# State-space steps of two groups taken as a pair, in a hybrid gMLP and Mamba-2 block

## The chip, the cores and the metric

The kernel runs on one core of one Trainium2 chip, in one launch. The metric is the device time of an execution in microseconds (us). An engine here is TensorE (PE, with its weight loads PEld), VectorE (DVE), ScalarE (ACT), GpSimd (POOL) or SyncE (SP); "SPq" and "ACTq" mark the instructions by which SP and ACT issue transfers.

## The reference

One layer of a trunk with two parallel branches, on x of 1024 positions by 1024 channels, in float32:

```python
h = rms_norm(x, norm_w) * (1 + scale) + shift          # scale, shift, gate from silu(c) @ ada_w + ada_b
gm_u, gm_v, gm_z, ssm_z, xbc, dt_raw, g_a, g_b = split(h @ w_in)
y_a = spatial_gating(gelu(gm_u), gelu(gm_v), ...) * silu(gm_z)
xs, bm, cm = split(silu(causal_depthwise_conv(xbc, conv_w, conv_b)))
dt = softplus(dt_raw + dt_bias);  a = -exp(a_log)
y_b = ssd_scan(xs, dt, a, bm, cm) + xs * d_skip         # 8 groups of 4 heads of 64, state 128, chunks of 128
y_b = rms_norm(y_b * silu(ssm_z))                       # by group of 256 channels
out = rms_norm(x + gate * ((sigmoid(g_a) * (y_a @ w_proj_a) + sigmoid(g_b) * (y_b @ w_proj_b)) @ w_out))
```

The part that the change touches is `ssd_scan`. For each group, chunk by chunk, with `decay` the masked exponential of differences of the cumulated `dt * a`:

```python
cb      = C_chunk @ B_chunk^T                           # 128 x 128, one for the group's 4 heads
y_diag  = (cb * decay[head]) @ xd[head]                 # inside the chunk
state   = state * chunk_decay + B_chunk^T @ (decay_to_end * xd)
y_off   = (C_chunk @ state_before) * exp(a_cs)          # from earlier chunks
```

## The kernel before

**Layout.** Everything is kept transposed, channels on partitions and positions along the free axis. The large projections are float32 products split into high and low parts (three products each) and combined in a scheme of seven products in place of eight. The state-space part comes near the end of the program, from about 920 to 1130 us. It is followed by the projection of branch B (tiles `x0p`, `x1p`, ..., the first of which are fed by `yn0`, `yn1`, ... on lines 1614 and 1651) and the output projection.

**One step.** A step is a group g and a pair of chunks s (256 positions). There are 8 groups and 4 pairs of chunks, so 32 steps. `order` runs them in rounds of two groups: (0,0), (1,0), (0,1), (1,1), (0,2), ... In the profile a tile's name has no numbers; in the order lists `yi5_0` is the tile of group 5, pair of chunks 0. A step does this:

- `fetch`: SP loads `dcy` (cumulated sums, spread over partitions, 512 KB) and `sl` (the slabs of C, B, x and gate, 768 KB). Five sets of buffers rotate.
- `mask`, `decay`: ACT makes `ea` (exponentials for y_off), POOL masks `dcy` (L1123), and ACT takes the eight exponentials of `dcy` (L1131).
- `prep`: PE makes `pc` (C·B, and B transposed) and `px` (x transposed). DVE multiplies `dcy` by `pc` (L1147) and makes `xd` and `xe` from `px` (L1150). ACT copies `bn`.
- `front`: PE makes `yi` (the part inside the chunk, eight products that are 64 columns wide, so that two heads share a bank), and `sp` (two increments of the state). DVE adds an increment to the state that POOL has multiplied by the chunk's decay (`st`, L1192 and L1200), and adds the skip term to `yi` (`y`, L1180).
- `back`: PE makes `yn` from the earlier states. DVE multiplies it by `ea` (`ym`, L1226), POOL adds and gates (L1228, L1229).

After each second step of a group, ACT stores the gated tile `yz` to `yb_d` (L94) and later squares it in place, so the squares wait until the store has read it. POOL adds the two halves (L1255 `sum`, or L1247 in `late_squares` for the last two groups), PE sums over partitions with a matrix of ones (`pq`, 32 columns wide), DVE scales the row (`cwt` or `tri`), ACT stores it to `ms_d`, SP loads it back as `ssq`, and POOL raises it to the power -1/2 (`root`).

**What fills PE between.** `proj_a`, the projection of branch A, is a generator of units, each of two 128x512 products (tiles `pma`). `draw(n)` takes n units. Its results are gated on DVE (`tha`, L1488) and stored by ACT to `mt_d` (L1490).

**What sets the order.** A scheduler places instructions, but the lists are mostly fixed by hand: `link` chains the instructions of ACT, DVE and POOL in the order in which they are written, products and loads are pinned in program order, `later(d, f)` runs f after d more calls of `run_tasks`, and `work` holds POOL's sums and roots, one of which `beside_step` takes. PSUM is eight banks: `bank` takes each from a ring of six (`bk`), or, every fourth time, from a ring of two (`px`). The loop over steps writes front, state product, fill, back, prep of step n+2, fetch of step n+5:

## Time and profile before

| | |
|---|---|
| Time, median of 3 runs | 1369.64 us (1369.3 to 1369.72) |
| The profiled execution | 1367.94 us, of which the span of the profile is 1366.0 us |
| Granted TensorE clock of that execution | 0.999 |
| PE busy | 1352.3 us (99%) |
| PEld, DVE, ACT, POOL busy | 82%, 77%, 59%, 14% of the span |
| Instructions of the span | 20176 |

Busy time is the share of a span in which an engine has an instruction running; the rows of the trace give for each group of instructions the start, the duration, the engine, the line, and the tiles as out<-in. Duration and distance from one start to the next are not the same: PE, DVE and ACT start an instruction while the one before is still ending. A matmul of float32 operands appears as two records, so the eight products of a `yi` are 16 records. Brackets name the idle time ahead of a row and what ended it. The profiled execution is 1.70 us under the median of the timed runs.

### The profile page before, as it was taken

How to read it: one execution, taken by the hardware profiler on the slowest of the kernel's cores; microseconds unless marked ns; L12 is line 12 of the kernel's file. 1: busy time of each engine (PE TensorE's matmuls, PEld its weight loads, DVE VectorE, ACT ScalarE, POOL GpSimd, SP SyncE). 2: the span in 40 equal slices, each digit the busy share in tenths (PEclk: the TensorE clock that was granted, in tenths of full speed). 3: DMA queues.
4: the chain of work that ended last, by engine and by line, in shares of the span. 5: the costliest groups of instructions: out<-in, count | busy, mean ns of one | idle time of the engine just before them, and what ended most of it. 6: DMA issues, size and time to landing. Idle time of an engine off the chain costs nothing.

```text
span 1366.0 us, 20176 instructions
## 1 busy us (share of the span) xinstructions
PE 1352.3 (99%) x6943; PEld 1116.6 (82%) x6943; DVE 1045.9 (77%) x1716; ACT 799.2 (59%) x1447; POOL 192.5 (14%) x191
## 2 busy tenths in 40 slices
PE   8999999999999999999999999999999999999997
PEld 7688888888888888888888888888888887888886
DVE  4786876777778888697887797458888866859976
ACT  5763666666666656466566556486877834233443
POOL 1000000000000000000000000006798971000002
PEclk9999999999999999999999999999999999999999
DMA  9674444334344657877656675589889959988903
GB/s 286 181 244 135 142 124 120 104 117 124 108 139 139 181 181 230 252 230 241 211 180 189 219 247 167 166 282 314 305 299 307 309 201 320 325 268 322 382 37 124
DMA packets 249530, 288.65 MB, mean 211 GB/s; under 512 B 16812, under 2 KB 196436, under 8 KB 249428
## 3 DMA queue, kind: packets, MB, share of 16 engines
q1 hardware_dynamic: 174868, 203.80, 46.9%
q10 hardware_dynamic: 74560, 83.57, 17.9%
q8 instruction: 55, 0.90, 0.3%
q14 instruction: 47, 0.39, 0.1%
HBM read 199.82 MB, written 87.49 MB: 210 GB/s over the span
## 4 chain that ended last, share of the span: by engine, by line
PE 92%; DMA 3%; DVE 2%; ACT 1%; SPq 1%; issue 0%; POOL 0%; POOLq 0%; DVEq 0%; ACTq 0%
PE xz L565 6%; PE xcb L565 6%; PE xx L565 6%; PE pma L82 6%; PE xuz L565 6%; PE xg L565 6%; PE ox L1867 3%; PE ycb L565 3%; PE vx L954 3%; PE yp L1676 3%; PE yz L565 3%; PE yx L565 3%; PE yg L565 3%; PE yuz L565 3%; PE yi L82 2%; PE sp L82 2%
## 5 line engine op out<-in xcount | busy, mean ns | idle before, releaser
L1123 POOL TENSOR_SCALAR_AFFINE_SELECT dcy<-dcy 128x1024 f32<-128x1024 f32 x32 | 35.3, 1103 | 790.6 <-ACT ea L1119 786.9
L1131 ACT ACTIVATE dcy<-dcy,nacs 128x128 f32<-128x128 f32 x256 | 78.3, 389 | 2.7 <-POOL dcy L1123 2.1
L1147 DVE TENSOR_TENSOR dcy<-dcy,pc 128x1024 f32<-128x1024 f32 x32 | 39.0, 1218 | 8.0 <-PE pc L85 6.4
L1229 POOL TENSOR_TENSOR yz<-y,sl 128x512 f32<-128x512 f32 x32 | 44.4, 1387 | 2.5
L82 PE MATMUL pma<-yh,wah 128*128 128x512 f32 x128 | 43.1, 418 | 0.0
L82 PE MATMUL pma<-yh,wal 128*128 128x512 f32 x128 | 42.5, 413 | 0.0
L82 PE MATMUL pma<-yl,wah 128*128 128x512 f32 x128 | 40.2, 396 | 0.0
L1119 ACT ACTIVATE ea<-dcy 64x512 f32<-64x512 f32 x64 | 39.8, 622 | 0.7 <-DMA dcy<-acs_d 0.3
L1024 ACT ACTIVATE ac<-ac 128x1024 f32<-128x1024 f32 x32 | 33.9, 1061 | 10.2 <-DVE ac L1022 10.0
L1614 DVE SCALAR_TENSOR_TENSOR yn<-yn,par,rb 128x512 f32<-128x512 f32 x32 | 25.4, 793 | 18.6 <-DMA yn<-yb_d 16.9
L1154 ACT COPY bn<-pc 128x256 f32<-128x256 f32 x32 | 11.9, 371 | 46.9 <-DVE dcy L1147 46.9
L1228 POOL TENSOR_TENSOR y<-y,ym 128x512 f32<-128x512 f32 (+1 forms) x32 | 37.0, 1155 | 1.9 <-DVE ym L1226 1.9
L1022 DVE SCALAR_TENSOR_TENSOR ac<-c2x,cwt,ac 128x1023 f32<-128x1023 f32 (+2 forms) x24 | 30.7, 1279 | 6.1 <-ACT ac L1020 6.0
L82 PE MATMUL yi<-dcy,xd 128*64 128x128 f32 x512 | 35.0, 279 | 0.0
L1022 DVE SCALAR_TENSOR_TENSOR ac<-c2cb,cwt,ac 128x1023 f32<-128x1023 f32 (+2 forms) x24 | 30.6, 1274 | 5.6 <-ACT ac L1020 5.5
L1882 POOL TENSOR_TENSOR r<-r,fnw 128x512 f32<-128x512 f32 x4 | 5.3, 1344 | 204.8 <-ACT junk L1880 204.8
L986 ACT ACTIVATE vm<-vm,vr 128x128 f32<-128x128 f32 x64 | 25.8, 484 | 14.2 <-DMA vm<-v_d 13.7
L1226 DVE TENSOR_TENSOR ym<-yn,ea 128x512 f32<-128x512 f32 (+1 forms) x32 | 19.9, 622 | 18.5 <-PE yn L82 18.4
L824 ACT CAST wbb<-wbr 128x512 fp32r<-128x512 f32 x32 | 19.8, 619 | 22.8 <-DMA wb_d<-wbb 17.0
L82 PE MATMUL sp<-xe,bn 128*128 128x256 f32 x112 | 32.7, 409 | 0.0
L82 PEld LDWEIGHTS yn<-sl,st 128*128 128x128 f32 x224 | 29.7, 191 | 2.8 <-POOL st L1192 0.4
L82 PEld LDWEIGHTS yi<-dcy,xd 128*64 128x64 f32 x512 | 27.3, 136 | 5.7 <-issue 3.1
(2963 smaller groups left out, 4372.8 us busy)
## 6 DMA issues: line engine op xcount, KB each, us to landing
sl<-s_d SPq DMA_DIRECT2D x32, 768.0 KB, 6.4
s_d<-ac ACTq DMA_DIRECT2D x32, 512.0 KB, 3.3
wb_d<-wbb ACTq DMA_DIRECT2D x32, 512.0 KB, 3.4
dcy<-acs_d SPq DMA_DIRECT2D x32, 512.0 KB, 5.3
av<-in_w_in_dram SPq DMA_DIRECT2D x36, 256.0 KB, 2.9
aw<-in_ada_w_dram SPq DMA_DIRECT2D x16, 512.0 KB, 6.6
wbr<-in_w_proj_b_dram SPq DMA_DIRECT2D x32, 256.0 KB, 5.1
yb_d<-yz ACTq DMA_DIRECT2D x32, 256.0 KB, 6.0
```

The lines of the kernel that those rows point to most:

```text
L82: pin(PE.matmul(acc, l, r, start=first, stop=last))
L565: pin(PE.matmul(ps, lw[:, k * P : (k + 1) * P], r[k], start=first and n + k == 0, stop=n == 2 and k == 3, skip_group_check=not first))
L954: pin(PE.matmul(ps[pn][j], l[:, j * P : (j + 1) * P], r, start=nm in ("p1", "p5", "p2") and n + units[i][1] == 0, stop=n == 2 and k == 3, ...
L1022: V.scalar_tensor_tensor(ac[:, s:], cc[:, : S - s], conv_wt[:, 3 - s, i : i + 1], ac[:, s:], op0=ALU.mult, op1=ALU.add)
L1119: link("A", lambda: A.activation(ea[hh * HD : (hh + 1) * HD], dcy.rearrange("p (j e) i l -> p e j (i l)", e=2)[hh * HD : (hh + 1) * HD, hh ...
L1123: link("G", lambda: G.affine_select(out=d8, in_=d8, compare_op=ALU.is_ge, fill=-1e30, base=0, pattern=[[0, 2 * HPG], [1, P]], channel_mult ...
L1131: link("A", lambda: A.activation(dcy[:, h, i, :], dcy[:, h, i, :], AF.Exp, bias=sub[:, i, h : h + 1]))
L1147: link("V", lambda: V.tensor_tensor(d3, d3, pc[:, 0:256].unsqueeze(1).to_broadcast([P, HPG, 256]), op=ALU.mult))
L1228: link("G", lambda: G.tensor_add(y1[:, :, t0:], y1[:, :, t0:], m[:, :, t0:]))
L1229: link("G", lambda: G.tensor_mul(yz, y1, sl[:, 4:6]))
L1676: pin(PE.matmul(ps[j], a[:, v, js], r, start=first and n + k == 0, stop=n == 2 and k == KT - 1, skip_group_check=not first))
L1867: pin(PE.matmul(ps, a[:, tsl], b[:, cs], start=first and n + j == 0, stop=n == 2 and j == 3, skip_group_check=not first))
```

## The change

Steps n and n+1 (the same pair of chunks of both groups of a round) are taken as one. `fronts` writes, on every engine's list, the inside products of both, then both rows of sums (`pq`), both increments, both skips, both first state additions, then the second state product and addition of the first group (`second`). POOL's sums or roots follow, two in a row, and the fill. `backs` writes both `yn` with the second group's second state product between, and both state products for the next pair. `preps` writes both `prep` of the next pair, both pairs of `ea` exponentials, both masks, and only then both `xe` (`prep2`). `fetch` is split: the loads of sums (`dcy`) are issued in `fronts`, those of `sl` at the pair's end. The squares come six slots after the store in place of eight, and the names of three PSUM banks of the next stage change places. No instruction is added or removed.

```diff
@@ fetch, exps, mask @@
-        def fetch(self, s):
-            g, nm = self.g, f"{self.g}_{s}"
-            n = nstep[0] % NSET
+        def fetch_sums(self, s):
...
+        def fetch(self, s):
...
+        def exps(self, s):
@@ prep @@
-            for v, f in (("xd", dthq), ("xe", dde)):
+            xd = scaled("xd", dthq)
...
+            self.rest = lambda: scaled("xe", dde)
+
+        def prep2(self, s):
+            self.pre[s][4] = self.rest()
@@ front, cut in three: inside (yi), increments (sp), skip (y) @@
-        def front(self, s):
+        def inside(self, s):
...
+        def increments(self, s):
...
+        def skip(self, s):
@@ post @@
-                later(8, self.squares, q, [yz[:, j] for j in range(2)])
+                later(6, self.squares, q, [yz[:, j] for j in range(2)])
@@ the loop @@
-    draw(6)
-    for n in range(2):
-        step(n, "front")
-        ahead_of(n)
-        draw(10)
-    for n in range(len(order)):
-        if n > 1:
-            step(n, "front")
-            ahead_of(n)
-            draw(6 if n == 2 else 4 + n % 2)
-        step(n, "back")
-        if n == 1:
-            draw(4)
-        if n + 2 < len(order):
-            step(n + 2, "prep")
-        fetch(n + 6)
+    def fronts(n):
+        decays(n + 4)
+        each(n, "inside")
+        while posts:
+            p, q, sq = posts.pop(0)
+            p.post2(q, sq)
+        each(n, "increments")
+        each(n, "skip")
+        each(n, "add_state", 0)
+        second(n)
+        upto("fetch_sums", n + 7)
+    def second(n):
+        g, s = order[n]
+        if s < NCH // 2 - 1:
+            groups[g].mul_state(s, 1)
+            groups[g].add_state(s, 1)
+    def backs(n):
+        for m in (n, n + 1):
+            g, s = order[m]
+            groups[g].back(s)
+            if m == n:
+                second(n + 1)
+            groups[g].close(s)
+        if n + 2 < len(order) and order[n + 2][1]:
+            each(n + 2, "mul_state", 0)
+    def preps(n):
+        for m in (n, n + 1):
+            if m < len(order):
+                g, s = order[m]
+                groups[g].prep(s)
+                upto("exps", m + 3)
+        upto("mask", n + 4)
+        each(n, "prep2")
+    draw(12)
+    for n in range(0, len(order), 2):
+        item(fronts, n)
         with tc.high_priority():
-            decays(n + 3)
...
+            for _ in range(2 if n < 28 else 4):
                 beside_step()
+        draw(4 if n == 0 else 3)
+        item(backs, n)
+        item(preps, n + 2)
+        upto("fetch", n + 7)
+        run_tasks()
+        draw(12 if n == 0 else 6 + n // 2 % 3 % 2)
+        run_tasks()
```

**PE, the step of group 4 and of group 5 at pair of chunks 0.** Before, from the products inside the chunk of step (5,0) to the next such products; `pq3_0` is a row of sums of group 3, `pma4_0` and `pma4_1` are fill, and eight fill rows like the two shown stand between them and `yn5_0`:

```order
L82 MATMUL yi5_0_9725<-dcy5_0_9403,xd5_0_9627 64x128 x8
L82 MATMUL pq3_0_9734<-yz3_0_9119,ones_140 32x128 x4
L82 MATMUL sp5_0_9741<-xe5_0_9629,bn5_0_9631 128x256 x2
L82 MATMUL pma4_0_9683<-yh10_8034,wah4_0_9361 128x512
L82 MATMUL pma4_1_9686<-yh11_8035,wah4_0_9361 128x512
```

Now, the same place:

```order
L82 MATMUL yi4_0_9647<-dcy4_0_9201,xd4_0_9578 64x128 x8
L82 MATMUL yi5_0_9656<-dcy5_0_9377,xd5_0_9596 64x128 x8
L82 MATMUL pq2_0_9665<-yz2_0_9064,ones_140 32x128 x4
L82 MATMUL pq3_0_9672<-yz3_0_9072,ones_140 32x128 x4
L82 MATMUL sp4_0_9679<-xe4_0_9609,bn4_0_9580 128x256 x2
L82 MATMUL sp5_0_9682<-xe5_0_9611,bn5_0_9598 128x256 x2
```

Both groups' narrow products stand in a row, as do both rows of sums and both pairs of increments. After them come 6 fill products, both `yn`, both `pc` and `px`, and 12 or 14 more fill products.

**SP, the loads ahead of group 5's first step.** Before (`ssq<-ms_d0` and `ssq<-ms_d1` read back the sums of groups 0 and 1):

```order
L91 DMA ssq_158<-ms_d0_66 128x8
L91 DMA dcy4_0_9315<-acs_d_57 128x1024
L91 DMA sl4_0_9317<-s_d4_125 128x1536
L91 DMA ssq_158<-ms_d1_67 128x8
L91 DMA dcy5_0_9403<-acs_d_57 128x1024
L91 DMA sl5_0_9405<-s_d5_126 128x1536
```

Now:

```order
L91 DMA dcy5_0_9377<-acs_d_57 128x1024
L91 DMA dcy4_1_9379<-acs_d_57 128x1024
L91 DMA ssq_158<-ms_d0_66 128x8
L91 DMA ssq_158<-ms_d1_67 128x8
L91 DMA sl5_0_9463<-s_d5_126 128x1536
L91 DMA sl4_1_9465<-s_d4_125 128x1536
```

The load of `sl4_0` has moved ahead of both reads of sums; `sl5_0` and `sl4_1` stand behind both. The next round has the same piece with groups 7 and 6.

**DVE and ACT at the stage's end.** On DVE, from the last `ym` (group 7, pair 3), before; `yn0_0` on line 1614 is the first operand of projection B, normalised after a load from `yb_d`:

```order
L1226 TENSOR_TENSOR ym7_3_10842<-yn7_3_10837,ea7_3_10531 128x512
L1488 SCALAR_TENSOR_TENSOR tha6_0_10576<-tha6_0_10576,pma6_0_10578 128x512
L1488 SCALAR_TENSOR_TENSOR tha6_1_10579<-tha6_1_10579,pma6_1_10581 128x512
L1267 TENSOR_SCALAR cwt_148<-pq6_0_10863 128x128
L1267 TENSOR_SCALAR tri_142<-pq7_0_10870 128x128
L1614 SCALAR_TENSOR_TENSOR yn0_0_10922<-yn0_0_10922,par2_147,rb0_0_10920 128x512
```

Now:

```order
L1239 TENSOR_TENSOR ym7_3_10831<-yn7_3_10826,ea7_3_10582 128x512
L1658 SCALAR_TENSOR_TENSOR yn0_0_10922<-yn0_0_10922,par2_147,rb0_0_10920 128x512
L1506 SCALAR_TENSOR_TENSOR tha6_0_10603<-tha6_0_10603,pma6_0_10605 128x512
L1506 SCALAR_TENSOR_TENSOR tha6_1_10606<-tha6_1_10606,pma6_1_10608 128x512
L1280 TENSOR_SCALAR cwt_148<-pq6_0_10871 128x128
L1280 TENSOR_SCALAR tri_142<-pq7_0_10878 128x128
```

`yn0_0` has moved ahead of the two `tha6`. On ACT, before, from the stores of group 6's last tile:

```order
L94 DMA yb_d12_103<-yz6_2_10679 128x512
L94 DMA yb_d13_104<-yz6_2_10679 128x512
L1490 DMA mt_d6_89<-tha6_0_10576 128x512
L1490 DMA mt_d6_89<-tha6_1_10579 128x512
L1268 DMA ms_d6_72<-cwt_148 4x128
L94 DMA yb_d14_105<-yz7_2_10749 128x512
L94 DMA yb_d15_106<-yz7_2_10749 128x512
L1268 DMA ms_d7_73<-tri_142 4x128
L1246 ACTIVATE yz6_2_10679<-yz6_2_10679 128x512 x2
```

Now:

```order
L1508 DMA mt_d6_89<-tha6_0_10603 128x512
L94 DMA yb_d12_103<-yz6_2_10704 128x512
L94 DMA yb_d13_104<-yz6_2_10704 128x512
L1508 DMA mt_d6_89<-tha6_1_10606 128x512
L1259 ACTIVATE yz6_2_10704<-yz6_2_10704 128x512
L1281 DMA ms_d6_72<-cwt_148 4x128
L94 DMA yb_d14_105<-yz7_2_10714 128x512
L94 DMA yb_d15_106<-yz7_2_10714 128x512
L1259 ACTIVATE yz6_2_10704<-yz6_2_10704 128x512
```

The store of the first `tha6` stands ahead of the stores of `yz6`, and the first square of `yz6` ahead of the stores of `yz7`.

More of the change, by code (lines that the diff above doesn't have):

```diff
@@ L1320, in start_ssd @@
             later(4 + 5 * n, decays, n + 1)
-            g, s = order[n]
-            later(13 + n, groups[g].prep, s)
+            later(13 + n, prep, n)
     def stats():
@@ L1797, in hybrid_kernel @@
             if nm == "p1":
-                first = {t: psb.tile([P, 512], F32, name=f"{t}p", tag=f"b{t}") for t in ('x0', 'x1', 'x2', 'y3', 'y0', 'y1', 'y2', 'x3')}
+                first = {t: psb.tile([P, 512], F32, name=f"{t}p", tag=f"b{t}") for t in ('x0', 'x1', 'x2', 'y2', 'y0', 'y3', 'y1', 'x3')}
                 psx, psy = ([first[f"{v}{j}"] for j in range(4)] for v in "xy")
```

106 lines of the change are left out of this document (52 added, 54 removed).

## The prediction

> **What bounds the kernel now.** I read the page first, then PE's waits, then single steps on PE, then each place where the change writes a wait that is not there today. The page's busy line and its chain of waits:
>
> ```profile
> PE 1352.3 (99%) x6943; PEld 1116.6 (82%) x6943; DVE 1045.9 (77%) x1716; ACT 799.2 (59%) x1447; POOL 192.5 (14%) x191
> PE 92%; DMA 3%; DVE 2%; ACT 1%; SPq 1%; issue 0%; POOL 0%; POOLq 0%; DVEq 0%; ACTq 0%
> ```
>
> PE is the bound. PE's waits over the whole state-space stage and its end (935 to 1140 us) are one row:
>
> ```profile
> PE pq L82 <- POOL yz L1247: 1.4, 2, 0.8
> ```
>
> So nothing in the steps holds PE up. It waits twice at the end, 1.4 us in all, for POOL's add of the last squares. Two things follow. A reordering can gain only what PE itself spends on the order of its products, and 1.4. And every wait that it writes into PE's list is paid in full, since PE has no idle time to absorb it.
>
> **What PE spends on changes of shape.** The timeline of PE in one step, as start, duration and records (two records to a product):
>
> ```profile
> 1042.36 1.05 PE L82 MATMUL yn<-sl,st 128*128 128x128 f32 x8
> 1043.25 0.39 PE L82 MATMUL pc<-sl 128*128 128x128 f32 x2
> ...
> 1044.13 0.38 PE L85 MATMUL px<-ident,sl 128*128 128x128 f32 x2
> 1044.44 1.09 PE L82 MATMUL yi<-dcy,xd 128*64 128x128 f32 x16
> 1045.46 0.43 PE L82 MATMUL pq<-yz,ones 128*32 128x128 f32 x8
> 1045.82 1.13 PE L82 MATMUL sp<-xe,bn 128*128 128x256 f32 x4
> 1046.60 0.81 PE L82 MATMUL pma<-yh,wal 128*128 128x512 f32 x2
> 1047.25 0.62 PE L82 MATMUL pma<-yh,wah 128*128 128x512 f32 x2
> 1047.71 0.62 PE L82 MATMUL pma<-yl,wah 128*128 128x512 f32 x2
> ```
>
> Narrower windows on the same step show how long the rows are when cut at 4 and at 12 records, and the first `sp` alone:
>
> ```profile
> 1044.44 0.44 PE L82 MATMUL yi<-dcy,xd 128*64 128x128 f32 x4
> 1044.44 0.88 PE L82 MATMUL yi<-dcy,xd 128*64 128x128 f32 x12
> 1045.82 0.48 PE L82 MATMUL sp<-xe,bn 128*128 128x256 f32 x1
> ```
>
> Eight records of `yi` take 0.88 - 0.44 = 0.44, so 16 at that pace take 0.88, and the episode takes 1.02 (1044.44 to 1045.46): 0.14 over. The two `px` records start 1044.13 and, at half of the 0.22 that two such take, 1044.24; `yi` comes 0.20 later in place of 0.11: 0.09 over. Behind it, `sp` goes at (1.13 - 0.48) / 3 = 0.217 a record and two `pma` records take 0.46 (1047.25 to 1047.71); from 1045.82 to 1047.25 that is 1.32, and it took 1.43: 0.11 over. A narrow episode thus costs 0.34 beyond its products. There are 32, and there will be 16:
>
> 16 x 0.34 = 5.5 us less.
>
> Rows of sums: alone, `pq` takes 0.36 (1045.46 to 1045.82). Where two stand in a row today,
>
> ```profile
> 1116.09 0.65 PE L82 MATMUL pq<-yz,ones 128*32 128x128 f32 x16
> 1116.66 0.74 PE L82 MATMUL pma<-yl,wah 128*128 128x512 f32 x2
> ```
>
> they take 0.57, which is 0.15 less than two apart. Six more meet: 0.9 less. **Together -6.4 us.** The products themselves are the same, so their sum moves by nothing.
>
> **What the new order writes into the middle: loads.** `sl5_0` was issued at 1004.62, and the transfer's median is 6.4:
>
> ```profile
> 1004.62 0.32 SPq L91 DMA_DIRECT2D sl<-s_d  x1
> ```
>
> ```profile
> sl<-s_d SPq DMA_DIRECT2D x32, 768.0 KB, 6.4
> ```
>
> PE uses it for `pc5_0` at 1018.85, and for `pc4_0` one step sooner:
>
> ```profile
> 1012.55 0.39 PE L82 MATMUL pc<-sl 128*128 128x128 f32 x2
> ...
> 1013.75 1.09 PE L82 MATMUL yi<-dcy,xd 128*64 128x128 f32 x16
> ...
> 1018.85 0.39 PE L82 MATMUL pc<-sl 128*128 128x128 f32 x2
> ```
>
> It landed about 1011.0, 7.8 ahead of its use. In the pair, `pc5_0` follows `pc4_0` by 1.2 (1012.55 to 1013.75) and not by 6.3, so it comes 5.1 sooner. Its load stays behind both reads of `ms_d`, and the store that the second read waits for now stands on ACT behind 16 exponentials and not 8, one row of which is
>
> ```profile
> 1004.52 2.44 ACT L1131 ACTIVATE dcy<-dcy,nacs 128x128 f32<-128x128 f32 x8
> ```
>
> That leaves 7.8 - 5.1 - 2.4 = 0.3. SP's own waits say how much such a read can slip:
>
> ```profile
> SPq L91 <- DMA ms_d<-tri: 2.3, 2, 1.4
> ```
>
> A slip of 1.4 is 1.1 late. It happens at groups 5 and 7: 2.2, with ends at 0 and, with a further 2.4 of exponentials ahead, 5. Behind the blocked read, `sl4_1` and the next `dcy` wait too; they are needed a pair later.
>
> **State products.** POOL's list now has two roots (or two sums) between the two groups' second state products. The groups by line for 935 to 1115:
>
> ```profile
> L1192 POOL TENSOR_TENSOR st<-st,cd 128x256 f32<-128x256 f32 x45 | 26.8, 613 | 3.7 <-DVE st L1200 2.8 <-DVE st L1198 0.7
> ...
> L1282 POOL TENSOR_TENSOR ssq<-ssq,nhalf 128x8 f32<-128x8 f32 x6 | 9.9, 1653 | 0.0
> ```
>
> ```profile
> L1147 DVE TENSOR_TENSOR dcy<-dcy,pc 128x1024 f32<-128x1024 f32 x29 | 35.4, 1219 | 7.5 <-PE pc L85 6.0 <-ACT ea L1119 0.7 <-issue 0.4
> ...
> L1150 DVE TENSOR_TENSOR xd<-px,dthq 128x512 f32<-128x512 f32 x29 | 19.8, 682 | 0.0
> L1150 DVE TENSOR_TENSOR xe<-px,dde 128x512 f32<-128x512 f32 x29 | 19.7, 680 | 0.0
> L1200 DVE TENSOR_TENSOR st<-st,sp 128x256 f32<-128x256 f32 x46 | 19.0, 414 | 6.8 <-POOL st L1192 5.6 <-PE sp L82 1.0
> ```
>
> From the end of `sp`: two additions 0.8, product 0.6, two roots 3.3, product 0.6, addition 0.4: 5.7 until `sp`'s bank is free. PE has 6 fill products at 0.23 (1.4), both `yn` (2 x 0.89, as from 1042.36 to 1043.25) and the first `pc` (1.2) until a `pc` takes that bank: 4.4. So 1.3 late, in the two rounds that take roots: 2.6. Ends: 0, where the bank falls to another tile, and 4.6, where the sums (shorter than the roots) hold three pairs more by 0.65 each.
>
> **Late `xe`.** Both `xe` now follow both groups' `dcy` and `xd`. By the rows above that is 2 x 1.22 + 4 x 0.68 = 5.2 after the first `pc` is done, so 6.4 after its start. PE is back at `yi` after 2.4 and 12 to 14 fill products (2.8 to 3.2), 5.2 to 5.6. A `yi` that takes a bank in which a `px` stood waits about 1.0; I count two such pairs, 2.0, ends 0 and 6. DVE issues a little before the last one ends, which speaks for the low side.
>
> **Sum of the middle: 2.2 + 2.6 + 2.0 = 6.8 us.**
>
> **The stage's end.** I take T as 1114.99, when the last `yn` is issued in full and the fill after it starts. The rows of before on PE, ACT, DVE, POOL and SP:
>
> ```profile
> 1114.99 0.71 PE L82 MATMUL pma<-yh,wal 128*128 128x512 f32 x2
> ...
> 1124.37 0.43 PE L82 MATMUL pq<-yz,ones 128*32 128x128 f32 x8 [0.57 <-POOL yz L1247]
> ...
> 1128.17 0.42 PE L82 MATMUL pq<-yz,ones 128*32 128x128 f32 x8 [0.84 <-POOL yz L1247]
> ...
> 1130.02 0.39 PE L1676 MATMUL x0p<-p1bh,p1a 128*128 128x512 f32 x1
> ```
>
> ```profile
> 1119.27 0.98 ACTq L94 DMA_DIRECT2D yb_d<-yz  x2
> ...
> 1124.92 0.63 ACT L1246 ACTIVATE yz<-yz 128x512 f32<-128x512 f32 x1 [1.96 <-DMA yb_d<-yz]
> ```
>
> ```profile
> 1115.88 1.27 DVE L1488 SCALAR_TENSOR_TENSOR tha<-tha,pma 128x512 f32<-128x512 f32 x2
> ...
> 1119.28 0.75 DVE L1614 SCALAR_TENSOR_TENSOR yn<-yn,par,rb 128x512 f32<-128x512 f32 x1 [1.73 <-issue]
> ```
>
> ```profile
> 1123.04 1.28 POOL L1247 TENSOR_TENSOR yz<-yz 128x512 f32<-128x512 f32 x1 [4.33 <-ACT yz L1246]
> ```
>
> ```profile
> 1115.27 0.32 SPq L91 DMA_DIRECT2D yn<-yb_d  x1
> ```
>
> Today `x0p` starts at T + 15.0. The load of `yn0_0` is issued at 1115.27 and used at 1119.28, 4.0 later; a store from issue to the square that waits for it takes 5.65. In the new lists the first `tha6` stands behind `yn0_0`, its store ahead of the stores of `yz6`, and the first square of `yz6` ahead of those of `yz7`. So: `yn0_0` done T + 5.0, `tha6` 5.7, stores of `yz6` issued by 6.2, landed 11.85, square 12.5, three ACT issues and the second square 14.3, POOL's add 15.6. PE has 16 fill products, two rows of sums and 28 fill products ahead of `pq6_1`, at 3.7 + 0.6 + 6.4 = T + 10.7: it waits 4.9. Then `yz7`: stores issued 13.0, landed 18.65, squares until 20.6, add 22.0. PE comes there after 10 fill products, T + 18.3: it waits 3.7. Six more fill products and `x0p` starts at T + 23.8. Ten fill products more than before lie behind T (60 in place of 50), worth 2.3, so **the end loses 23.8 - 2.3 - 15.0 = 6.5 us**. Ends: 4, if a store takes 1.2 less both times, and 8.5, if it takes 1 more.
>
> The Trainium skill, on the page "DMA: Bandwidth & Descriptors", section "Anatomy of one DMA — SWDGE (gpsimd) path", fits a transfer as 2.0 us and its bytes over 436 GB/s. A transfer of 256 KB would take 2.6 by that fit, an estimate from the page; worked through the same chain, the two rows of sums would wait 0.4 and 0.8, the end would win 0.9, and the total would come to about 1369. The rows disagree, at 4.0 and 5.65 under this load, and they decide.
>
> **The forecast.** -6.4 + 6.8 + 6.5 = +6.9 us on the profiled execution's 1367.94, so 1374.8; that execution is 1.7 under the median of the runs, 1369.64, and on the median the same +6.9 gives 1376.5. A measurement of this kernel can tell about 0.2% (2.7 us) from no change.
>
> **The rivals.**
>
> *Only the shape changes count (faster).* PE waits for nothing in today's steps, which speaks for slack that the middle does not exhaust; the waits of the middle then come to 0. It decides for faster if the stores at the end also land some 3 us sooner, so that the two late rows of sums wait 0 to 3 us more than now and not 6.5. Then -6.4 + 0 to 3: 1363 to 1366.5, middle 1365. Against it: the order at the end is written in the program, and each link has a measured row.
>
> *A wash.* The end loses its 6.5 and the middle nothing: 1369.64 - 6.4 + 6.5 = 1369.7, within 2.7.
>
> *POOL or DVE becomes the bound of each pair (slower still).* The places above hold all 16 pairs and not a few: 14 pairs by a further 0.6 us, as the excess of a sum over PE's time (0.65) suggests, is 8 more, 1384 to 1385. For it: the second group's state, `xe` and `yn` queue behind the first group's on in-order engines. Against it: `st` on DVE waited only 5.6 for POOL in 180 us, so both have some time left.
>
> **How the numbers follow.** The forecast, +3 to +12, has 0.62. Only shapes 0.19, wash 0.09, POOL or DVE 0.10. Faster is the first rival, 0.19; same is the wash, 0.09; slower is the forecast and the last rival, 0.72. The range is 1364 to 1383: below it lies a part of the first rival, above it most of the last and the sum of the terms' upper ends (5 + 4.6 + 6 + 8.5 - 6.4 = +17.7), which I hold for less than 1 in 10 to be reached together.
>
> **What would show it.** Right: 16 narrow episodes of about 1.9 us; PE's waits name `pq <- POOL yz` with 4 to 5 and 3 to 4 us, a `pc <- DMA sl` of 1 to 2 near groups 5 and 7, and a few of about 1 us for DVE's `st` or `xe`, 15 us in all. Wrong: `pq` waits under 2 in all, or middle waits under 2 (then the time is 1365 to 1370), or waits at every pair (then over 1383). If the narrow episodes of the pair are no shorter than two of today's, the 6.4 was not there to gain.

## The result and the profile after

The changed kernel takes 1382.49 us (median of 6 runs, 1381.97 to 1388.64), and the kernel before took 1369.68 beside it (median of 6, 1367.75 to 1371.89). The ratio is 1.0102 [1.0089, 1.0116]: 12.8 us slower, where 6.9 were forecast. The sign and the range hold; the size was nearly twice the forecast. In the experiments below a kernel's ratio is its time over that of the kernel before on the same chip, with its 95% interval.

The profiled execution took 1384.35 us with a span of 1382.6, 1.9 above the median. The page's busy line for it (engine, busy time, share, instructions):

```profile
PE 1354.8 (98%) x6943; PEld 1119.4 (81%) x6943; DVE 1044.2 (76%) x1716; ACT 798.7 (58%) x1447; POOL 190.9 (14%) x191
```

PE has the same 6943 records of products and is busy 2.5 us longer; the rest of the 16.6 us by which the span grew is idle time. PE's waits from 900 to 1150 us name it (total, times, longest):

```profile
PE pc L82 <- DVE st L1210: 2.9, 1, 2.9
PE pq L82 <- POOL yz L1260: 2.8, 1, 2.8
PE px L85 <- DVE st L1210: 2.4, 2, 1.5
PE yi L82 <- DVE xe L1155: 1.6, 2, 1.1
PE yi L82 <- ACT ea L1121: 1.3, 1, 1.3
PE yn L82 <- DVE st L1208: 0.8, 1, 0.8
PE yn L82 <- DVE st L1210: 0.7, 1, 0.7
PE sp L82 <- ACT bn L1161: 0.6, 1, 0.6
PE yi L82 <- POOL st L1201: 0.6, 1, 0.6
```

Where before had two waits of 1.4 us together, there are now eleven of 13.8. All but the `pq` lie in the stage; no row names a load of `sl`. PE's timeline of after has the marks and the places (start, duration, records, and the idle time ahead with what ended it):

```profile
910.95 0.38 PE L82 MATMUL pc<-sl 128*128 128x128 f32 x2
...
1024.84 1.97 PE L82 MATMUL yi<-dcy,xd 128*64 128x128 f32 x32
1026.73 0.65 PE L82 MATMUL pq<-yz,ones 128*32 128x128 f32 x16
...
1035.62 0.69 PE L82 MATMUL pc<-sl 128*128 128x128 f32 x2 [2.94 <-DVE st L1210]
...
1124.99 0.71 PE L82 MATMUL pma<-yh,wah 128*128 128x512 f32 x2
1125.53 0.63 PE L82 MATMUL pma<-yl,wah 128*128 128x512 f32 x2
...
1138.86 0.66 PE L82 MATMUL pq<-yz,ones 128*32 128x128 f32 x8 [2.78 <-POOL yz L1260]
...
1140.47 1.05 PE L82 MATMUL pma<-yh,wal 128*128 128x512 f32 x2
1141.32 1.05 PE L82 MATMUL pma<-yh,wah 128*128 128x512 f32 x2
...
1146.25 0.39 PE L1720 MATMUL x0p<-p1bh,p1a 128*128 128x512 f32 x1
```

Between the first `pc` and T (the fill behind the last `yn`, as in the prediction) before took 207.34 us and after 214.04; from T to `x0p` 15.02 and 21.26; from `x0p` to the start of PE's last product 229.11 and 229.12. Ten fill products, worth 2.3 us, moved from the stage to its end, so the reordering cost 6.7 + 2.3 = 9.0 in the stage and 6.2 - 2.3 = 3.9 at its end. Of the remaining 3.6 us or so, 0.3 lie behind PE's last product and 3.3 ahead of the stage, in code that the change leaves alone: there the granted clock fell in this execution (the row for 24 to 32 us below has 0.79, and before has 1.00), which is 1.7 of the 3.3. The median is 1.9 us lower than this execution.

The last two fill rows above start 0.85 apart; undisturbed pairs start 0.46 apart. The windows of after (start and end, length, busy time of the five engines, granted clock, DMA share, GB/s) explain it:

```profile
24.00:32.00 8.00, 7.26 (x44) 4.66 (x47) 4.50 (x11) 3.96 (x8) 0.10 (x1) 0.79 0.93 238
...
1036.00:1037.00 1.00, 1.00 (x7) 1.00 (x7) 1.00 (x2) 0.00 (x0) 0.92 (x2) 0.50 1.07 391
1140.00:1145.00 5.00, 5.00 (x19) 3.25 (x18) 3.46 (x4) 3.29 (x6) 1.28 (x1) 0.50 0.89 295
```

The first row stands ahead of the stage, the others in it. Behind the wait of 2.94 the clock is at half for 3.4 us. At the wait of 2.78 it is at half for 6.8 us, from 1138.2 on; the wait itself lasts until 1138.86, so 0.7 of the 6.8 fall into idle time and cost nothing. Before shows 1.00 in 1020 to 1040 and in 1120 to 1140. Half of 3.4 is 1.7 us and half of 6.1 is 3.1: 4.8 us together, not much less than the two waits (5.7).

Where the 2.94 comes from, in the timelines of POOL, DVE and ACT of after:

```profile
1029.56 3.28 POOL L1295 TENSOR_TENSOR ssq<-ssq,nhalf 128x8 f32<-128x8 f32 x2
1032.80 0.61 POOL L1201 TENSOR_TENSOR st<-st,cd 128x256 f32<-128x256 f32 x1
```

```profile
1034.54 0.69 DVE L1400 TENSOR_TENSOR wal<-wa,wah 128x512 fp32r<-128x512 f32 x1 [3.22 <-ACT wah L1395]
1035.15 0.41 DVE L1210 TENSOR_TENSOR st<-st,sp 128x256 f32<-128x256 f32 x1
```

```profile
1033.91 0.60 ACT L1395 CAST wah<-wa 128x512 fp32r<-128x512 f32 x1
```

The second group's state product ends at 33.4, behind two roots. Its addition on DVE could follow at once, but a step of the fill's weights (`wal`) stands ahead of it on DVE, and that waits for ACT's cast until 34.5. Read from these rows, the roots make about 1.2 of the 2.94 and the cast 1.7. In the next round, at groups 6 and 7, two roots stand on POOL in the same way, but `wal` has run before them, and the addition follows the product at once:

```profile
1087.38 0.42 DVE L1210 TENSOR_TENSOR st<-st,sp 128x256 f32<-128x256 f32 x1 [2.73 <-POOL st L1201]
```

There PE waits 0.88, one of the two waits of `px`.

The stage's end, in the timelines of ACT, DVE and POOL of after:

```profile
1129.91 0.88 ACTq L94 DMA_DIRECT2D yb_d<-yz  x2
...
1135.25 0.63 ACT L1259 ACTIVATE yz<-yz 128x512 f32<-128x512 f32 x1 [16.77 <-DMA yb_d<-yz]
```

```profile
1127.99 0.75 DVE L1658 SCALAR_TENSOR_TENSOR yn<-yn,par,rb 128x512 f32<-128x512 f32 x1 [2.03 <-DMA yn<-yb_d]
```

```profile
1123.50 3.26 POOL L1295 TENSOR_TENSOR ssq<-ssq,nhalf 128x8 f32<-128x8 f32 x2
1126.72 1.29 POOL L1241 TENSOR_TENSOR y<-y,ym 128x512 f32<-128x512 f32 x1
```

`yn0_0` does stand ahead of the `tha6`, as forecast, but its load took 2.7 us (issued 1125.26) and not 4.0. The store of `yz6` took 5.3 (1129.91 to 1135.25), near the 5.65. And two roots stand ahead of the last products of `yz6` on POOL, which the prediction did not speak of: the tile is ready 4.9 us after T, when the store of the first `tha6` is already out.

### The profile page after: what moved, and what is told of

Read it like the earlier page. It is cut to its first block, busy times and chain, and to the rows that moved or that the text cites. A ratio compares the mean times of both kernels' runs of the same rounds, so it can differ in the third digit from the quotient of the medians.

```text
span 1382.6 us, 20261 instructions
## 1 busy us (share of the span) xinstructions
PE 1354.8 (98%) x6943; PEld 1119.4 (81%) x6943; DVE 1044.2 (76%) x1716; ACT 798.7 (58%) x1447; POOL 190.9 (14%) x191
## 3 DMA queue, kind: packets, MB, share of 16 engines
q10 hardware_dynamic: 74560, 83.57, 17.7%
## 5 line engine op out<-in xcount | busy, mean ns | idle before, releaser
L82 PE MATMUL yi<-dcy,xd 128*64 128x128 f32 x512 | 31.9, 276 | 3.6 <-DVE xe L1155 1.6
L1210 DVE TENSOR_TENSOR st<-st,sp 128x256 f32<-128x256 f32 x48 | 19.0, 416 | 21.3 <-POOL st L1201 18.1
L1192 DVE SCALAR_TENSOR_TENSOR y<-sl,dskt,yi 128x256 f32<-128x256 f32 x64 | 27.2, 475 | 6.3 <-POOL dcy L1128 2.5
L1201 POOL TENSOR_TENSOR st<-st,cd 128x256 f32<-128x256 f32 x48 | 29.8, 633 | 13.7 <-DVE st L1210 4.7
L1022 DVE SCALAR_TENSOR_TENSOR ac<-c1cb,cwt,ac 128x1023 f32<-128x1023 f32 (+2 forms) x24 | 30.7, 1278 | 1.3 <-ACT ac L1020 1.3
```

The costliest lines, as they stand in the source:

```text
L82: pin(PE.matmul(acc, l, r, start=first, stop=last))
L1022: V.scalar_tensor_tensor(ac[:, s:], cc[:, : S - s], conv_wt[:, 3 - s, i : i + 1], ac[:, s:], op0=ALU.mult, op1=ALU.add)
L1201: link("G", lambda: G.tensor_mul(v3(self.next), v3(self.st), fac(cd, self.g, s)[:, i].unsqueeze(2).to_broadcast([P, HPG, HD])))
```

## The experiments

The theory after the result: each wait is written by the place of an instruction on an in-order list, PE pays it in full, and a wait of some 3 us is paid again in clock. The rival: DVE, POOL or the loads are simply late in a pair, so that a moved instruction only hands its wait to the next. Three kernels change the second states, two the end, one the `xe`, one measures the price of a change of shape, two put an amount of delay into the kernel before, and the rest join what helped. Stage is first `pc` to T, end is T to `x0p`, both read from PE's timeline of the profiled execution. Fill is drawn in units of two products. The fill's steps `wah` and `wal` are not on the hand-made lists: the scheduler places them, so an edit can move them too.

| kernel | ratio to before | stage | end | half clock behind waits |
|---|---|---|---|---|
| before | 1 | 207.3 | 15.0 | none |
| after | 1.0102 [1.0089, 1.0116] | 214.0 | 21.3 | stage and end |
| p_add | 1.0145 [1.0124, 1.0166] | 220.7 | 21.5 | end |
| p_mul | 1.0036 [1.0023, 1.0049] | 210.7 | 22.1 | stage and end |
| p_both4 | 1.0031 [1.0019, 1.0044] | 205.9 | 21.2 | end |
| p_end2 | 1.0069 [1.0052, 1.0086] | 214.2 | 17.9 | stage |
| p_end3 | 1.0047 [1.0032, 1.0062] | 214.6 | 17.0 | stage |
| x_xe | 1.0070 [1.0057, 1.0083] | 211.3 | 19.6 | stage |
| s_split | 1.0098 [1.0085, 1.0112] | 219.9 | 17.0 | end |
| c_k1 | 1.0033 [1.0021, 1.0046] | 207.4 | 16.4 | none |
| c_k3 | 1.0059 [1.0047, 1.0072] | 207.3 | 23.3 | end |
| b_end | 1.0023 [1.0014, 1.0032] | 205.9 | 17.4 | none |
| b_all | 1.0060 [1.0047, 1.0072] | 204.4 | 17.8 | behind the end |
| b_all8 | 1.0216 [1.0202, 1.0230] | 223.0 | 20.8 | four places |
| b_endxe3 | 1.0019 [1.0006, 1.0031] | 210.7 | 18.8 | stage |
| b_all3 | 1.0008 [0.9996, 1.0019] | 208.4 | 17.7 | stage |

Kernels with the pair have ten fill products more in the end and ten fewer in the stage than before, s_split, c_k1 and c_k3.

**p_add: the second group's state ahead of the fill.** Of after:

```diff
     def backs(n):
...
-            if m == n:
-                second(n + 1)
...
+        item2(second, n + 1)      # behind the roots, ahead of draw()
```

> The changed kernel, with only the second group's state addition (DVE) taken ahead of the fill, so that DVE does not stand at the fill's cast wal (which waits for ACT) before it; POOL's list is as in the changed kernel. In its trace the wait of pc at groups 4 and 5 is 2.94 us, and the granted clock is 0.50 for 3.4 us behind it. Theory A (DVE's list: the cast ahead of the addition adds 1.7 us to what POOL's roots make late, and an idle time near 3 us halves the clock): that wait falls to about 1.2, the clock stays 1.00 there, and the time is 3 to 4 us less than the changed kernel's (+12.8 us over before becomes about +9.5). Theory B (POOL's two roots alone make that wait): it stays near 2.9, nothing changes, about +12.8. What my prediction would say: 1.3 us in the wait and no effect of the clock.

From PE's waits in p_add, and DVE's row ahead of the addition that `pc` waits for:

```profile
PE yn L82 <- DVE st L1210: 12.1, 9, 2.7
...
PE pc L82 <- DVE st L1210: 1.7, 1, 1.7
```

```profile
1033.39 0.72 DVE L1400 TENSOR_TENSOR wal<-wa,wah 128x512 fp32r<-128x512 f32 x1 [1.91 <-ACT wah L1395]
```

The `pc` waits 1.7 in place of 2.9, but not for the reason that was expected: at this place `wal` still stands ahead of the addition, which starts at 1034.04. The cast came sooner in this kernel, so `wal` adds about 0.5 behind the end of the product (1033.57) and not 1.7. And `yn` waits nine times, so the time is 20.5 us over before, where 9.5 were expected. The second states rotate through three buffers. Moved ahead of `yn`, the second group's new state goes into the buffer from which the first group's `yn` of the same pair should still read, and `yn` now waits for that write (in this kernel and in p_mul a part of the output is thus computed from an overwritten state). So the place of `second(n + 1)` in after was tied to the buffers, and this run mixes two edits. p_both4 parts them.

**p_mul: only the product moves.** It goes ahead of the roots, the addition stays where `second(n + 1)` was:

```diff
     def fronts(n):
...
+        if order[n + 1][1] < NCH // 2 - 1:
+            groups[order[n + 1][0]].mul_state(order[n + 1][1], 1)
...
     def backs(n):
...
-            if m == n:
-                second(n + 1)
+            if m == n and order[n + 1][1] < NCH // 2 - 1:
+                groups[order[n + 1][0]].add_state(order[n + 1][1], 1)
```

> The changed kernel, with only the second group's state product (POOL) taken ahead of POOL's two sums or roots; the addition on DVE stays where it is. Theory A (DVE's cast in front of the addition holds it just as long): the wait of pc near groups 4 and 5 stays over 2 us, and if it stays under about 2.5 the clock may stay at 1.00; time 0 to 2 us less than the changed kernel's, +11 to +13 over before. Theory B (POOL's roots alone): the wait of 2.94 goes, the half clock with it, and also 0.88 of px near groups 6 and 7: 5 to 6 us less, about +7.

From PE's waits in p_mul:

```profile
PE yn L82 <- POOL st L1201: 2.1, 4, 0.7
PE yn L82 <- DVE st L1210: 1.6, 1, 1.6
```

The `pc` wait is gone, and the stage 3.3 us shorter than in after. The time is 5.0 us over before, nearer to theory B. But the run does not part roots from cast: at this place the scheduler also put `wal` behind the addition (1033.02 and 1030.56), so both causes went. The write of the product makes `yn` wait (2.1). The 1.6 stands at the last pair of groups 2 and 3, where first additions stand behind a `wal` that waits 2.5 for ACT; in after that place costs 0.7.

**p_both4: the whole second state in `fronts`, with a fourth buffer.**

```diff
-            bn = p2x.tile([P, 256], F32, name=f"bn{nm}", tag="bn", bufs=3)
+            bn = p2x.tile([P, 256], F32, name=f"bn{nm}", tag="bn", bufs=2)
-            self.next = (st1[n % 2], st2[n % 3])[i]
+            self.next = (st1[n % 2], st2[n % 4])[i]
...
         second(n)
+        second(n + 1)
         upto("fetch_sums", n + 7)
...
-            if m == n:
-                second(n + 1)
```

> The changed kernel, with the second group's state product and addition written right behind the first group's, ahead of POOL's two sums or roots and of the fill's casts. So that no state is overwritten before yn has read it, the second states rotate over four buffers, not three (bn gets two buffers, not three, to make room). Theory A (the second group's state stands behind POOL's roots and DVE's cast): the waits of pc near groups 4 and 5 (2.94 us in the changed kernel's trace) and of px near groups 6 and 7 (0.88) go, and the half clock behind the first (3.4 us at 0.50, 1.7 lost) with them: 5 to 6 us less than the changed kernel's, +7 to +8 over before. The rest of its waits stay. Theory B (the first group's state or the banks are what is waited for): the waits stay within 0.5 us, +12 to +13.

From PE's waits in p_both4:

```profile
PE pq L82 <- POOL yz L1260: 4.0, 2, 3.6
```

No `pc` waits, and the granted clock stays at 1.00 behind that place (1030 to 1040 us). Here too `wal` runs behind the addition. The stage takes 205.9, 8.1 less than in after: its waits come to 4.7 in place of 11.0, and 1.7 of clock is saved. With the 2.3 us of fill that moved, the stage is 0.9 longer than before. The time is 4.7 us over before, less than the 7 to 8 expected, because some waits went that were to stay (the 1.3 for `ea` among them). The order on POOL and DVE made this part of the loss: the same work on the same engines takes less time in another order. The end is as late as in after.

**p_end2: `tha6` and `yn0_0` back in their old order.**

```diff
-            keep = pin if dd == KT - 1 else lambda i: i
+            keep = pin if dd >= KT - 2 else lambda i: i
...
+        keep = pin if (n, h) == (0, 0) else lambda i: i
+        keep(V.scalar_tensor_tensor(t, t, snw[:, n : n + 1], rbs[n // 2, h], op0=ALU.mult, op1=ALU.mult))
```

> The changed kernel, with only the first operand of projection B (yn0_0 on DVE) kept behind the two tha6, as in the kernel before; both stores of tha6 then go out together. This undoes the step on which my prediction rested for the end. Theory P (the prediction's: the load of yn0_0 delays tha6, its store the stores of yz6, and so the last rows of sums): the wait of pq falls from 2.8 us to under 1, and with it goes the half clock behind it (6.8 us at 0.50, 3.4 us lost): 4 to 6 us less than the changed kernel's, about +7.5 over before. Theory E (POOL: the roots of groups 4 and 5 stand ahead of the last pair's y and yz, and yz6 is ready only when the store is issued, 4.9 us after the last yn): nothing or under 0.5 us, +12.3 to +13.

From ACT's timeline at the end of p_end2:

```profile
1126.48 0.92 ACTq L94 DMA_DIRECT2D yb_d<-yz  x2
...
1129.28 0.63 ACT L1259 ACTIVATE yz<-yz 128x512 f32<-128x512 f32 x1 [13.87 <-DMA yb_d<-yz]
```

The time is 8.6 us over before, near the 7.5 of theory P. The end takes 3.4 us less, with no half clock from 1120 to 1142; `pq` waits 0.4 and 1.6. The order of two DVE instructions was a cause, as the prediction said, but not by its path: the stores of `yz6` are issued 4.6 us after T and not 4.9, while the same store landed in 2.8 us where after needed 5.3. What made it land sooner is not shown.

**p_end3: the last two roots behind the last products of `yz`.**

```diff
-            for _ in range(2 if n < 28 else 4):
+            for _ in range(2):
```

> The changed kernel, with POOL's two roots of groups 4 and 5 taken behind the last pair's y and yz and not ahead of them (two sums or roots a pair in the last two pairs too, in place of four). Theory E (POOL makes the end late): yz6 is ready about 3 us after the last yn in place of 4.9, its squares follow, the wait of pq falls from 2.8 to under 0.5 and the clock stays at 1.00: 5 to 6 us less than the changed kernel's, about +7 over before. Theory P (yn0_0 ahead of tha6): under 1 us, about +12.

From PE's waits in p_end3:

```profile
PE pq L82 <- POOL yz L1260: 1.2, 1, 1.2
```

This alone does as much: the time is 6.6 us over before, near the 7 of theory E, and the end takes 17.0. `yz6` is ready 2.9 us after T and not 4.9. Part is lost again behind `x0p` (231.5 us to the last product, 229.1 in after). Two causes stood in a row, and removing either leaves shorter waits with no fall of the clock behind them.

**x_xe: each `xe` behind its own `xd`.**

```diff
                 groups[g].prep(s)
+                groups[g].prep2(s)
                 upto("exps", m + 3)
         upto("mask", n + 4)
-        each(n, "prep2")
```

> The changed kernel, with each xe written right behind its own xd as in the kernel before, and not behind both groups' dcy and xd. My prediction counted 2.0 us for two pairs in which yi takes a bank that a px held. In the changed kernel's trace the waits of yi for xe are 0.52 and 1.07. Theory: both waits fall under 0.3, the stage (from the first pc to the end of the last yn, 214.0 us there) is 1.5 to 2 us shorter, about +11 over before. Rival (the second group's dcy and xd then come 0.6 us later and their yi waits in its place): the stage changes by under 0.5.

From PE's waits in x_xe, and the second group's state product on POOL and its addition on DVE at groups 4 and 5:

```profile
PE pc L82 <- DVE st L1210: 1.2, 1, 1.2
```

```profile
1031.53 0.61 POOL L1201 TENSOR_TENSOR st<-st,cd 128x256 f32<-128x256 f32 x1
```

```profile
1032.17 0.42 DVE L1210 TENSOR_TENSOR st<-st,sp 128x256 f32<-128x256 f32 x1 [2.14 <-POOL st L1201]
```

The two `xe` waits of 0.5 and 1.1 went, and one of 1.3 and one of 0.6 for `xd` came: the rival is right for this part, the wait is handed on. That the `pc` waits 1.2 and not 2.9 was not expected. The rows say why: the roots still stand ahead of the product, but `wal` has moved behind the addition (it runs at 1035.51), and the addition follows the product at once. So the roots alone cost 1.2 at this place, as read from the rows of after, and the other 1.7 was the cast. The time, 10.6 us over before, is near the +11 expected, but through this wait and not through the `xe`. The stage is 2.7 shorter, though a half-clock stretch appears at its start (0.89 from 920 to 935).

**s_split: the price of a change of shape.** The kernel before with one unit of fill put between the two halves of each `yi`, and one fewer in the draws:

```diff
+                if not i:
+                    draw(1)
...
-        draw(10)
+        draw(9)
...
-            draw(6 if n == 2 else 4 + n % 2)
+            draw(5 if n == 2 else 3 + n % 2)
```

> The kernel before, with each narrow episode yi cut in two: four products, one fill unit (two records' pairs of pma), four products; one fill unit fewer behind each step, so that the products are the same. It measures the price of an episode of narrow products without the pair. 32 episodes more. Theory of the prediction (0.34 us an episode: 0.09 at its entry, 0.14 within, 0.11 behind): +10.9 us over before, PE's waits as before. Rival (the gaps in the rows are the profile's modelled ends, and the change gained little by fewer episodes): under +4.

From PE's waits in s_split:

```profile
PE pq L82 <- POOL yz L1249: 1.9, 1, 1.9
PE yn L82 <- DVE st L1200: 0.3, 1, 0.3
```

The stage is 12.6 us longer with 32 more narrow episodes and 0.3 in waits (the 1.9 lies behind T): 12.26 over 32, 0.38 each. That is near the forecast of 0.34; the time is 13.8 us over before where 10.9 were expected, the rest of it at the end. By this price 16 episodes fewer would earn the pair 16 x 0.38 = 6.1, an estimate.

**c_k1 and c_k3: a known delay at the end of the kernel before.** POOL's last addition of squares of group 6 is done once or three times more (which alters that row of sums):

```diff
-            G.tensor_add(sq[0], sq[0], sq[1])
+            for _ in range(2 if self.g == NG - 2 else 1):    # in c_k3: 4
+                G.tensor_add(sq[0], sq[0], sq[1])
```

> The kernel before, with one more POOL add of 1.3 us ahead of group 6's last row of sums (the half is added twice, which alters that row of sums). The wait of pq for it is 0.57 us before and becomes about 1.9; the second wait (0.84) goes. Theory clock (an idle time of about 3 us halves the granted clock, a short one doesn't): clock 1.00 there, +0.5 us. Rival (any idle time over about 1 us does): 0.50 for some us behind it, +2 to +4.

> As c_k1 with three more adds: the wait of pq becomes about 4.5 us, the second wait goes. Theory clock: the clock falls to 0.50 for 3.4 or 6.8 us behind it, so the time grows by 3.1 (the waits) and 1.7 to 3.4 (the clock): +5 to +6.5. Rival (the clock in the changed kernel fell for another reason, and a wait costs its length): +3.1, clock 1.00.

PE's waits in c_k1 and in c_k3, then the windows behind each wait, with the granted clock in the column behind POOL's:

```profile
PE pq L82 <- POOL yz L1248: 2.9, 1, 2.9
```

```profile
PE pq L82 <- POOL yz L1248: 7.2, 1, 7.2
```

```profile
1130.00:1134.00 4.00, 4.00 (x25) 2.91 (x24) 2.22 (x5) 2.01 (x5) 0.00 (x0) 1.00 0.76 241
```

```profile
1128.00:1140.00 12.00, 6.92 (x31) 4.57 (x32) 7.65 (x12) 4.34 (x8) 4.49 (x3) 0.57 0.73 239
```

A wait of 2.93 with no fall of the clock behind it, and one of 7.2 with 0.57: over the 12 us that is 10.2 at half clock, 4.4 of them still inside the wait. The waits were larger than the additions' durations, so the size of a wait could not be set as finely as meant. c_k1 takes 4.8 us more than before, where 0.5 was expected: 1.4 at the end, and 3.4 behind `x0p` (232.5 in place of 229.1 to the last product), in waits for operands that come late. c_k3 takes 7.8 more, where 5 to 6.5 were expected. The stage itself does not move in either, so the added time stands behind it.

**b_end: p_both4, p_end2 and p_end3 together.**

> p_both4 (second states on four buffers, both groups' second state products and additions ahead of the roots and casts), p_end2 (yn0_0 behind the tha6) and p_end3 (the last two roots behind the last y and yz) together. If the three causes are separate: the stage as in p_both4 (205.9 us from first pc to last yn), the end as in p_end3 or shorter (17.0 us from last yn to the first product of projection B, with ten more fill products in it than before), the clock at 1.00, so 0 to +1.5 over before. If the end is held by something else (the stores' time): the end stays over 19 and the time over +3.

The window of b_end over stage and end:

```profile
900.00:1150.00 250.00, 242.73 (x1805) 205.91 (x1804) 200.94 (x341) 169.51 (x427) 175.02 (x166) 1.00 0.83 291
```

The clock is 1.00 over stage and end. Median 1371.5 beside 1368.12: 3.4 us of after's 12.8 remain (0 to 1.5 were expected), and so the three edits, each by order or by one buffer, take away about 9. The longest of the remaining waits is 1.05. From `x0p` to the last product it takes 230.5 in place of 229.1, since operands that were ready before are now waited for.

**b_all: `xe` early too, and six units of fill ahead of the first pair's `yn` in place of four.** Against b_end:

```diff
+                groups[g].prep2(s)
...
-        draw(4 if n == 0 else 3)
+        draw(6 if n == 0 else 3)
...
-        draw(12 if n == 0 else 6 + n // 2 % 3 % 2)
+        draw(10 if n == 0 else 6 + n // 2 % 3 % 2)
```

> b_end with xe behind its own xd, and with 6 and 10 units of fill in the first pair in place of 4 and 12 (its yn waits 0.84 us and its px 0.96 in p_both4). It would keep the saving on changes of shape (about 6 us) and lose what waits remain: 2 to 3 us less than b_end, -2.5 to 0 over before. If the waits only move to another engine: as b_end.

From PE's waits in b_all:

```profile
PE x2p L1720 <- DVE tha L1506: 5.7, 1, 5.7
```

It takes 8.4 us over before, where -2.5 to 0 were expected. The stage is 204.4, 1.5 less than b_end's, and then `x2p` waits 5.7 for the bank from which the last `tha` is added: the names of the next stage's banks are fixed, and a shifted fill meets the wrong one. So the three names in the change are part of the same order.

**b_all8: b_all with the squares again eight slots after the store.** Against b_all:

```diff
-                later(6, self.squares, q, [yz[:, j] for j in range(2)])
+                later(8, self.squares, q, [yz[:, j] for j in range(2)])
```

> b_all with the squares eight slots behind the store as in the kernel before, not six. In the changed kernel four squares stand on ACT ahead of both bn near groups 2 and 3, and sp waits 0.64 us for bn, then yn 0.74 for a state behind a cast that waits for ACT. If the squares cause them: both go, 1.3 us less than b_all. If not: as b_all within 0.5, or longer at the end, since the rows of sums come later.

At the place where `sp` waits 1.3 for `bn` in b_all it now waits 2.3 for `y` on DVE, and there are further new waits of up to 2.3; the clock falls in four places. Whether the squares, six slots on, hold `bn` is not shown by this run; putting them back is no way out.

**b_endxe3 and b_all3: names `x2` and `y2` exchanged.** The first is b_end with early `xe`, the second b_all:

```diff
...
-('x0', 'x1', 'x2', 'y2', 'y0', 'y3', 'y1', 'x3')
+('x0', 'x1', 'y2', 'x2', 'y0', 'y3', 'y1', 'x3')
...
```

> b_end with xe behind its own xd (the step of x_xe), and with two PSUM names of projection B's first product changed over (x2 and y2), so that x2p doesn't take the bank that the last tha still reads (in b_all x2p waited 5.7 us for it). If the account is right (16 episodes at 0.34 to 0.39 us and six row sums saved, and every wait paid in full): stage 204.5 to 205.5 us, end 17 to 17.8, no wait of x2p, and 0 to 2 us less than b_end's +3.1 over before. If the pair has a further cost that the waits don't show: as b_end or more.

> b_all with the same two names changed over. Its stage was 204.4 us in b_all's trace, its end 17.8, and 8.3 us went after that into x2p's wait (5.7, and the half clock behind it). Without that wait: b_all's +8.2 over before less 7.5 to 8.5, so -0.5 to +1. If the account misses something: over +3.

PE's wait in b_endxe3, and then that in b_all3 and the window behind it:

```profile
PE px L85 <- DVE st L1210: 4.2, 1, 4.2
```

```profile
PE px L85 <- DVE st L1210: 3.6, 1, 3.6
```

```profile
928.00:935.00 7.00, 5.63 (x22) 5.25 (x23) 6.67 (x11) 4.04 (x11) 5.97 (x8) 0.53 0.80 280
```

The wait of `x2p` is gone, as expected. Both got a new one at the stage's start, with 6.8 us at half clock, and take 3.3 and 1.7 us over before, more than expected. Still, b_all3 is level with before, so the pair's gain about pays for the waits that are left. What it would take without the wait of 3.6 was not run; two of its twelve executions had a granted clock of 0.999, as in before's profile, and took 1368.5 and 1369.9, which is 2.3 and 1.0 under before's median; the other ten took longer than these. Why a `px` that waits 1.0 to 1.5 in the other kernels with the pair waits 3.6 to 4.2 in these two stands on POOL in b_all3:

```profile
919.10 3.52 POOL L1128 TENSOR_SCALAR_AFFINE_SELECT dcy<-dcy 128x1024 f32<-128x1024 f32 x1 [18.62 <-ACT ea L1121]
```

This mask takes 1.09 in the fourteen other kernels, and there one of the fill's `yl` on DVE takes 1.55 and not 0.68. Here four `yl` run at 0.7 each (919.17 to 921.67), and the mask ends only behind them (922.62). ACT's exponentials, the casts and the additions then come some 2 us later. What lets one engine or the other go first is open. No version here beats the kernel before.

## Why the prediction was right in sign and wrong in size

- **PE is the bound and pays every wait.** Right. The page still has 98%, `x0p` to the last product is unchanged (229.1), and the time follows the waits.
- **Shapes, -6.4.** Right to about 1. Narrow products of a pair take 1.89 (1024.84 to 1026.73), two episodes of before 2 x 1.02. Split the other way, an episode costs 0.38. In b_all, the stage without its waits (3.9, and 0.17 more for each of the four, see below) and with the ten fill products put back is 5.3 shorter than before's.
- **"A slip of 1.4 is 1.1 late. It happens at groups 5 and 7: 2.2."** Wrong: no wait of PE names a load of `sl`. The term was 0, its lower end.
- **State products, 2.6.** The mechanism was right, and both places show: 0.88 at group 7's round, under the 1.3 forecast, and 2.94 at group 5's. The step that failed is "product 0.6, addition 0.4": it takes the addition to follow the product at once. At group 7's round it did, and in x_xe (1.25) at group 5's. In after the step `wal` of the fill stood between them at group 5's round and waited for ACT, 1.7. The prediction read POOL's list there and not DVE's.
- **Late `xe`, 2.0.** Nearly right: 0.5 and 1.1. But x_xe shows that the way out is not free.
- **"Sum of the middle: 6.8".** This is the step that was mis-sized. The waits of the stage come to 11.0. The places with a term make 5.4 of it (0 for loads, 3.8 for state products, 1.6 for `xe`). Six places had none, 5.6 together: 0.84 and 1.54 for states at the stage's start, 0.74 for a state behind `wal`, 0.64 for `bn` behind squares and exponentials on ACT, 0.56 for a state on POOL, and 1.26 for an `ea` on ACT. With 1.7 of clock and -6.4 of shapes that is 6.3 of the measured 9.0. Of the other 2.7, some 1.7 is that records overlap: the row at 1124.99 lasts 0.71 and the next starts after 0.54, so each idle gap reads about 0.17 short, 1.7 over ten gaps. The last 1.0 is what the shapes gave less than forecast. So the stage, forecast at -6.4 + 6.8 = +0.4, lost 9.0.
- **The end, 6.5.** 3.9 measured, and for another reason. The order of `yn0_0` and `tha6` counts (p_end2), but "two rows of sums wait 4.9 and 3.7" became 2.78 and none: the load took 2.7 in place of 4.0, the first store 5.3 and the second 4.4 in place of 5.65, and at half clock the fill between the two rows lasted longer, so the second row came late enough. The 2.6 us a transfer that the prediction set aside fits the load and neither store. With the 3.1 us of clock taken off, the end has lost about 0.8. POOL's roots were a second cause that was not in the chain (p_end3). The end was forecast 2.6 too high and the stage 8.6 too low; that the sum came no further off than it did is luck.
- **The clock.** Missing altogether: no term had it, and in stage and end it is 4.8 us of the profiled execution.
- **The rivals.** "Only the shape changes count" needed waits of 0 in the middle; b_all3, the nearest to it, is level and not faster. "POOL or DVE becomes the bound of each pair" did not come: waits stand at eleven places and not at sixteen, and p_both4 takes more than half of them away (11.0 to 4.7) by order and one buffer.

## What to carry to other kernels

Where one engine is full, first list, for each pair of producer and consumer that a reorder changes, everything that stands between them on every in-order list, the casts of unrelated work included. Count waits of about 3 us on the matrix engine twice, since the clock can halve behind them, and look at the clock by windows before reading a loss as work. Buffers that rotate and banks that are named are part of the order: moving an instruction past a reader or shifting the fill by two units needs another buffer or another name. And where a scheduler places part of the work, read the order that ran in the trace of each experiment: in p_mul and x_xe the cast moved unasked, and in p_add it stayed ahead of the addition that the edit was to bring past it.

## What the hardware showed that was not expected

In idle time of PE or up to 1.2 us behind it the granted clock falls to 0.50, for 3.4 us, 6.8, or 10.2 (c_k3). In the kernels here every wait of 3.1 us or more brought it (3.1 in p_end2, 3.6 in p_both4 and b_all3, 3.9 in p_mul, 4.1 in p_add, 4.2 in b_endxe3, 5.2 in b_all8, 5.7 in b_all, 7.2 in c_k3). Between 1.9 and 2.9 it happened or not: at 2.94 and 2.78 (after) and 1.9 (s_split) it fell, at 2.93 (c_k1), 2.7 (p_end3) and 2.6 (p_add, three times, and x_xe) it did not; in b_all8 it fell at 2.28 and 2.22 and not at another 2.28 and 2.17. In x_xe, p_mul and p_end3 it fell behind two waits of 0.85 and 0.95 within 3 us at the stage's start; in p_add, p_end2 and p_both4 it did not behind the same two, nor in after behind 0.84 and 1.54. The shortest single wait, in a window of s_split behind its 1.9:

```profile
1140.00:1141.00 1.00, 1.00 (x3) 0.72 (x3) 1.00 (x3) 1.00 (x3) 0.00 (x0) 0.50 1.09 346
```

The Trainium skill, on the page "TensorE: Matmul & The Clock Gate", section "What's actually happening", says that half clock is the state that comes back after at least one idle window of about 3.4 us, and that these windows run freely. The steps of 3.4, 6.8 and 10.2 us and the dependence on the moment agree with that. The falls after 1.9 to 2.9 us of idle time do not: that is less than one window. The runs do not show where the windows lie, so what decides between two waits of the same length stays open.
